# Twelve modulation units on another engine: from small TensorE matmuls in a scan loop to VectorE sums there and in the projection behind it

## The chip, the cores and the metric

The kernel runs on one core of a Trainium2 chip. The metric is the device time of one execution in microseconds (us), the median of the runs shown. The engines are named as in the profile: PE is TensorE (PEld its weight loads), DVE is VectorE, ACT is ScalarE, POOL is GpSimd and SP is SyncE, which here issues every load and store. All tensors are float32; large matmuls are made of three products of a rounded high part and a remainder (float32r).

## The reference, cut to what matters

Two transformer-like blocks over 256 positions of width 2048. In the first, a vector c is turned into six modulation rows of 2048 numbers, and these scale, shift and gate what follows:

```python
mod = jax.nn.silu(c) @ ada_w + ada_b
sh_m, sc_m, g_m, sh_f, sc_f, g_f = jnp.split((mod + ada_table[layer])[:, None, :], N_MOD, axis=-1)
h = _rms(x, norm_mix_pre[layer]) * (1 + sc_m) + sh_m
y, v_first = _rwkv7_mix(h, ...)
x = x + g_m * _rms(y, norm_mix_post[layer])
h = _rms(x, norm_ffn_pre[layer]) * (1 + sc_f) + sh_f
f = _conv_ffn(h, ...)
x = x + g_f * _rms(f, norm_ffn_post[layer])
```

`ada_w` has 2048 rows and 12288 columns, 100 MB in all. `_rwkv7_mix` projects h to r, k, v and some small hidden vectors, runs a recurrence with a 64 by 64 state for each of 32 heads over the 256 positions, and projects the outcome with `w_o`. `_conv_ffn` is a gated FFN of width 5504. The second block (attention, convolution and a gate) is not touched.

## The kernel before, in words

The program is written with a tile framework: the text allots tiles from pools, and the framework draws up each engine's queue, sets the semaphores and may take an instruction ahead of an earlier one whose operands or buffers are not free; what comes earlier in the text has the higher priority. So the order on an engine is near that of the text, but not the same.

**Modulation units.** A unit computes 512 columns of one modulation row (`k0` is the first of its four blocks of 128 columns; `seg` the row). A helper reads the 2048 x 512 part of `ada_w` in eight loads of 512 KB into the pool `adap` (three buffers in the stages that matter) and yields after every second load, so a unit has four steps. There are two helpers:

- `ada_group_pe` (lines 243 to 262) multiplies each 128 x 512 block on TensorE by a 128 x 32 tile whose first column is silu(c) (line 256, 16 matmuls a unit, two records each in the profile), copies the result from PSUM with ScalarE (line 260) and so makes a row.
- `ada_group` (lines 213 to 241) multiplies each block by silu(c) on VectorE and adds it to an accumulator `acc` of 128 x 512: the first block by line 232, the other 15 by line 238. Two other ways in it, on ScalarE and GpSimd, are switched off (`ada_pool[0] = 0`).

In both, `ada_fm` (lines 264 to 275) closes the unit: four matmuls with a column of ones (line 273) sum over the partitions into a column layout, and VectorE adds the bias (line 275). `ada_row` writes the 512 numbers to DRAM one by one (line 306), from where a later stage reads them as a row; `ada_scale` and `ada_shift` leave them in the tile `dv`. `ada_run(lag, ...)` chains units; it closes one when `lag` steps of the next have run, or at the next step when `lag` is 0.

**Stages.** First (to about 300 us) the norm, the modulation rows 0 and 1, and the k, v and low-rank products. Then the loop over q = 0 to 3 (lines 851 to 865), one pass for four pairs of heads:

```python
for i in range(4):
    for _ in operands(q * 4 + i, AR, BK, EC):
        for _ in range(SSTEP):
            next(sc, None)
        for _ in range(QSTEP):
            next(ada, None)
for _ in sc:
    pass
sc = scan(q, AR, BK, EC)
```

`operands` makes one pair's inputs of the scan and yields three times: after the low-rank part, after the r product (`fm_unit`, two `w_r` loads of 512 KB, split into high and remainder by ScalarE line 135 and VectorE line 139, 48 matmuls at lines 150 to 152), and at its end (lines 608 to 623). `scan(q)` runs as a generator beside the operands of pass q + 1: it starts with lines 690 and 693, solves 32 triangular systems by 30 serial steps of a multiply and an add on VectorE (lines 726 and 729), transposes (739, 742), and then goes through four chunks with matmuls, copies and a norm. `ada` is the run of twelve late units: rows 2 (units 0 to 3, the gate `g_m`, written to DRAM as `gmd`), 4 (units 4 to 7, scale of the FFN norm) and 3 (units 8 to 11, its shift). Before, each of the 48 yields takes one step, so all twelve units are done on TensorE in the loop.

After the loop, scan 3 runs beside `e_proj` and the first w_o products. The w_o product goes by four blocks `nb` of 512 columns (lines 980 to 998); `tm_out` evicts a block and multiplies it with the gate row `grow`, which is read back from `gmd` at line 994. Then come the residual (line 910), the norm, `to_fm` with the transposes, which needs the scales and shifts of units 4 to 11, and the FFN. In the FFN's loop over 43 blocks four more units (row 5, written as `gfd`) run with `ada_group` on VectorE, one step every third block.

Buffers: `NADA2 = 3` loads of `ada_w`, `NRAW = 4` weight loads and `NWHL = 2` splits in the loop, `NRAW2 = 5` and 3 afterwards.

Of the kernel before, what the change touches and what calls it, by code (L numbers as in the profile page):

```python
# [20 lines left out]
SSTEP, QSTEP = 3, 1  # L21
# [7 lines left out]
ADALAG = 2  # L29

GROUPS = ((0, 2), (2, 4), (6, 4), (10, 4), (14, 2))
P = 128
T = 256
D = 2048
KT = 16
# [23 lines left out]
def body(tc, A, out):  # L59
# [153 lines left out]
    def ada_group(seg, k0, nk, accs):  # L213
# [4 lines left out]
        for q in range(KT // n):  # L218
            raw = t_(adap[0], [P, 1024], "raw").rearrange("p (a c) -> p a c", c=w_)
            SP.dma_start(raw, A["ada_w"][q * n * P:(q + 1) * n * P, c0:c0 + w_].rearrange("(a p) c -> p a c", p=P))  # L220
            for a in range(n):
                b = q * n + a
                sc = sil[:, b:b + 1]
                w = 1 if b % 4 < ada_pool[0] else 0
                if accs[w] is None:
                    accs[w] = t_(accp[0], [P, 512], f"acc{w}", bufs=2 - w)
                acc = accs[w][:, :w_]
                if first[w]:
                    if w:
                        S.activation(acc, raw[:, a, :], AF.Copy, scale=sc)  # L230
                    else:
                        V.tensor_scalar(acc, raw[:, a, :], sc, None, op0=ALU.mult)
                elif w:
                    tp = t_(small, [P, 512], "nbr", bufs=1)[:, :w_]
                    S.activation(tp, raw[:, a, :], AF.Copy, scale=sc)
                    G.tensor_tensor(acc, acc, tp, op=ALU.add)
                else:
                    V.scalar_tensor_tensor(acc, raw[:, a, :], sc, acc, op0=ALU.mult, op1=ALU.add)
                first[w] = False
# [121 lines left out]
    def mix(m, k0, nk, dst, d0=0):  # L361

        mt = t_(pa, [P, 4, T], "mt", bufs=2)[:, :nk, :]
        for i in range(nk):
# [15 lines left out]
    ada = ada_run(ADALAG, *[ada_row(2, k0, 4, V_NMP, gmd) for k0 in range(0, KT, 4)],  # L380
                  *[ada_scale(4, k0, 4, D_AF, V_NFP) for k0 in range(0, KT, 4)],
                  *[ada_shift(3, k0, 4, D_BF) for k0 in range(0, KT, 4)])
# [146 lines left out]
    adap[0] = adx.enter_context(pool("adap2", NADA2, side="right"))  # L529
    phb = ExitStack()  # L530
# [16 lines left out]
    def operands(j, AR, BK, EC):  # L547

        w, i = divmod(j, 4)
        l2 = t_(pr, [P, 4, P], "l2", bufs=2)  # L550
# [300 lines left out]
    for q in range(4):  # L851
# [3 lines left out]
        for i in range(4):  # L855
            for _ in operands(q * 4 + i, AR, BK, EC):
                for _ in range(SSTEP):
                    next(sc, None)
                for _ in range(QSTEP):
                    next(ada, None)  # L860
# [3 lines left out]
    for _ in ada:  # L864
        pass
# [115 lines left out]
    for nb in range(4):  # L981
# [13 lines left out]
        elif nb == 1:  # L995
            V.tensor_copy(xt[:, 0, 0:1], accs(1)[0][:, 0:1])
            SP.dma_start(xt, A["x"].rearrange("(h p) d -> p h d", p=P))
        tm_out(po, accs(nb), nb, y2, grow, ssq)
# [13 lines left out]
    accp[0] = phf.enter_context(pool("accp", 2, reuse_waits="tile"))  # L1012
# [410 lines left out]
```

## Time and profile before

| | us |
|---|---|
| median of 3 runs | 2219.46 |
| lowest, highest | 2217.79, 2228.51 |
| the profiled execution's own time | 2202.98 |
| its span, first to last instruction | 2201.2 |

The profile is of one execution. Its page gives busy time by engine, the span in 40 slices with the granted TensorE clock, the DMA queues, the chain of work that ended last, and groups of instructions. In a group, "out<-in" names the tiles, "xcount" the instructions, then busy us and the mean ns of one, and behind the second bar the idle time of that engine just before them with what ended it. In the rows by stretches each engine has its busy us and, in brackets, its instructions; PEclk is the granted clock of TensorE as a share of 2.4 GHz, and the last two numbers are the DMA share and GB/s.

### The profile page before, as it was taken

The page shows a single profiled execution, that of the slowest core. Times are in us where ns is not written, and L with a number is a line of the kernel's source. Part 1 is how long each engine was busy: PE and PEld are TensorE (multiplying, and loading weights), DVE is VectorE, ACT ScalarE, POOL GpSimd, SP SyncE. Part 2 cuts the span into 40 slices and gives each one's busy share as a digit, 9 for nine tenths or more (in the row PEclk, how much of TensorE's full clock was granted, in tenths as well). Part 3 has the DMA queues.
Part 4 walks back from the last instruction along what each step waited for, and adds up shares of the span by engine and source line. Part 5 has one row for each costly group of instructions (what it writes and reads, how often), then busy time and mean ns, then how long its engine had stood idle before and what let it go on. Part 6 is the DMA issues. An engine that isn't in the chain of part 4 may idle for free.

```text
span 2201.2 us, 37566 instructions
## 1 busy us (share of the span) xinstructions
PE 2054.0 (93%) x15092; PEld 1728.1 (79%) x15092; DVE 1312.3 (60%) x2229; ACT 1001.7 (46%) x1554; POOL 387.7 (18%) x210
## 2 busy tenths in 40 slices
PE   6999977699999899799999999999998999999998
PEld 3778854466666467699999999978886889998887
DVE  3687873757676657866567676523336476665435
ACT  3544462234343444545544545434445444454453
POOL 1000000000000000122223222222332322322232
PEclk8999998889999989899999999999999999999999
DMA  8888656777664748665667566576664545556664
GB/s 291 297 297 283 206 199 205 200 200 217 197 209 152 207 150 303 212 193 180 185 183 248 181 213 190 175 233 193 191 196 135 177 144 175 170 165 219 191 197 153
DMA packets 192351, 446.36 MB, mean 203 GB/s; under 512 B 42792, under 2 KB 65448, under 8 KB 190896
## 3 DMA queue, kind: packets, MB, share of 16 engines
q1 hardware_dynamic: 192176, 443.96, 63.9%
q8 instruction: 118, 1.93, 0.4%
q14 instruction: 57, 0.47, 0.1%
HBM read 427.63 MB, written 16.27 MB: 202 GB/s over the span
## 4 chain that ended last, share of the span: by engine, by line
PE 81%; DMA 8%; DVE 6%; ACT 3%; issue 1%; SPq 0%; another core or an unknown queue 0%; POOL 0%; ACTq 0%; DVEq 0%; POOLq 0%
PE ps_s L150 6%; PE ps_s L152 6%; PE ps_s L151 6%; PE ps_g L150 5%; PE ps_g L152 5%; PE ps_g L151 5%; PE ps_a L256 4%; DMA raw<-in_ada_w 4%; PE ps_s L165 4%; PE ps_g L167 4%; PE ps_s L166 4%; PE ps_s L167 4%; PE ps_g L166 4%; PE ps_g L165 4%; DVE wlo L139 1%; PE ps_s L438 1%
## 5 line engine op out<-in xcount | busy, mean ns | idle before, releaser
L135 ACT ACTIVATE whi<-raw 128x1024 fp32r<-128x1024 f32 x562 | 594.0, 1058 | 741.7 <-issue 157.9
L139 DVE TENSOR_TENSOR wlo<-raw,whi 128x1024 fp32r<-128x1024 f32 x414 | 509.7, 1233 | 457.0 <-ACT whi L135 454.2
L139 POOL TENSOR_TENSOR wlo<-raw,whi 128x1024 fp32r<-128x1024 f32 x148 | 363.1, 2454 | 980.6 <-ACT whi L135 944.9
L150 PE MATMUL ps_g<-xh,whi 128*128 128x256 f32 x816 | 236.8, 290 | 14.7 <-ACT whi L135 14.7
L152 PE MATMUL ps_g<-xh,wlo 128*128 128x256 f32 x816 | 236.8, 290 | 3.0 <-DVE wlo L139 2.9
L151 PE MATMUL ps_g<-xl,whi 128*128 128x256 f32 x816 | 236.0, 289 | 0.0
L152 PE MATMUL ps_s<-xh,wlo 128*128 128x256 f32 x816 | 231.1, 283 | 2.7 <-DVE wlo L139 2.7
L150 PE MATMUL ps_s<-xh,whi 128*128 128x256 f32 x816 | 231.1, 283 | 0.0
L151 PE MATMUL ps_s<-xl,whi 128*128 128x256 f32 x816 | 230.9, 283 | 0.0
L150 PEld LDWEIGHTS ps_g<-xh,whi 128*128 128x128 f32 x816 | 160.5, 197 | 26.3 <-ACT whi L135 16.7
L256 PE MATMUL ps_a<-raw,sil 128*32 128x512 f32 (+1 forms) x704 | 139.7, 591 | 36.5 <-DMA raw<-in_ada_w 26.6
L152 PEld LDWEIGHTS ps_g<-xh,wlo 128*128 128x128 f32 x816 | 160.2, 196 | 13.0 <-issue 6.2
L151 PEld LDWEIGHTS ps_g<-xl,whi 128*128 128x128 f32 x816 | 160.4, 197 | 5.0 <-issue 4.2
L152 PEld LDWEIGHTS ps_s<-xh,wlo 128*128 128x128 f32 x816 | 156.6, 192 | 3.1 <-DVE wlo L139 3.1
L150 PEld LDWEIGHTS ps_s<-xh,whi 128*128 128x128 f32 x816 | 156.8, 192 | 0.0
L151 PEld LDWEIGHTS ps_s<-xl,whi 128*128 128x128 f32 x816 | 156.6, 192 | 0.0
L150 PE MATMUL ps_s<-h3h,whi 128*128 128x256 f32 x384 | 107.8, 281 | 0.0
L152 PE MATMUL ps_s<-h3h,wlo 128*128 128x256 f32 x384 | 106.6, 278 | 0.0
L151 PE MATMUL ps_s<-h3l,whi 128*128 128x256 f32 x384 | 106.2, 277 | 0.0
L256 PEld LDWEIGHTS ps_a<-raw,sil 128*32 128x32 f32 x704 | 23.3, 110 | 82.2 <-DMA raw<-in_ada_w 41.1
L150 PEld LDWEIGHTS ps_s<-h3h,whi 128*128 128x128 f32 x384 | 72.2, 188 | 3.6 <-issue 3.5
L152 PEld LDWEIGHTS ps_s<-h3h,wlo 128*128 128x128 f32 x384 | 72.3, 188 | 0.3 <-issue 0.3
(494 smaller groups left out, 4633.0 us busy)
## 6 DMA issues: line engine op xcount, KB each, us to landing
raw<-in_w_f SPq DMA_DIRECT2D x258, 512.0 KB, 4.5
raw<-in_ada_w SPq DMA_DIRECT2D x192, 512.0 KB, 5.4
raw<-in_w_i2f SPq DMA_DIRECT2D x80, 512.0 KB, 3.7
raw<-in_w_o SPq DMA_DIRECT2D x64, 512.0 KB, 4.8
raw<-in_w_v SPq DMA_DIRECT2D x32, 512.0 KB, 4.7
raw<-in_w_k SPq DMA_DIRECT2D x32, 512.0 KB, 4.8
raw<-in_w_r SPq DMA_DIRECT2D x32, 512.0 KB, 7.3
raw<-in_w_g SPq DMA_DIRECT2D x32, 512.0 KB, 4.8
```

The lines of the kernel that those rows point to most:

```text
L135: S.activation(hi, raw, AF.Copy)
L139: e.tensor_sub(lo, raw, hi)
L150: mm(acc, wh[:, sl], xh[:, kt, :], start=(kt == 0), stop=False)
L151: mm(acc, wh[:, sl], xl[:, kt, :], start=False, stop=False)
L152: mm(acc, wl[:, sl], xh[:, kt, :], start=False, stop=(kt == KT - 1))
L165: mm(a, xh, wh[:, sl], start=st, stop=False)
L166: mm(a, xl, wh[:, sl], start=False, stop=False)
L167: mm(a, xh, wl[:, sl], start=False, stop=sp_)
L256: mm(acc[r:r + 32, :w_], sil32[:, b, :], raw[:, a, :], start=(b < 4), stop=(b >= KT - 4))
L438: mm(acc[:, o], wl[:, sl], x[0][:, kt, :], start=False, stop=(i == 1 and kt == nk - 1))
```

## The change

All twelve late units use `ada_group` on VectorE (the list `ON_PE` of units that stay on TensorE is empty). In the loop over q only the first two of the three yields take a step, so 32 steps, eight units, remain there. The other four units take 4, 6 and 6 steps in the w_o product, ahead of the eviction of its blocks 0, 1 and 2. Their accumulator `acc` has one buffer, in a pool opened before the loop, and the FFN's four units use the same one, where they had a pool of their own with two. Units are closed at the next step (`ADALAG` 0 instead of 2). The small weight tile `l2` has one buffer instead of two.

```diff
-SSTEP, QSTEP = 3, 1
+SSTEP, QSTEP = 3, 2
+OSTEP = (4, 6, 6, 0)
+
+ON_PE = ()
...
-ADALAG = 2
+ADALAG = 0
...
-                    accs[w] = t_(accp[0], [P, 512], f"acc{w}", bufs=2 - w)
+                    accs[w] = t_(accp[0], [P, 512], f"acc{w}", bufs=1)
...
-    ada = ada_run(ADALAG, *[ada_row(2, k0, 4, V_NMP, gmd) for k0 in range(0, KT, 4)],
-                  *[ada_scale(4, k0, 4, D_AF, V_NFP) for k0 in range(0, KT, 4)],
-                  *[ada_shift(3, k0, 4, D_BF) for k0 in range(0, KT, 4)])
+    late = []
+    for u in range(12):
+        ada_how[0] = ada_group_pe if u in ON_PE else ada_group
+        k0 = u % 4 * 4
+        late.append(ada_row(2, k0, 4, V_NMP, gmd) if u < 4 else ada_scale(4, k0, 4, D_AF, V_NFP) if u < 8
+                    else ada_shift(3, k0, 4, D_BF))
+    ada = ada_run(ADALAG, *late)
...
     adap[0] = adx.enter_context(pool("adap2", NADA2, side="right"))
+    accp[0] = adx.enter_context(pool("accp", 1, side="right"))
...
-        l2 = t_(pr, [P, 4, P], "l2", bufs=2)
+        l2 = t_(pr, [P, 4, P], "l2")
...
-            for _ in operands(q * 4 + i, AR, BK, EC):
+            for e, _ in enumerate(operands(q * 4 + i, AR, BK, EC)):
                 for _ in range(SSTEP):
                     next(sc, None)
-                for _ in range(QSTEP):
+                if e < QSTEP:
                     next(ada, None)
...
-    for _ in ada:
-        pass
     wide_m[0] = True
...
+        for _ in range(OSTEP[nb]):
+            next(ada, None)
         tm_out(po, accs(nb), nb, y2, grow, ssq)
...
-    accp[0] = phf.enter_context(pool("accp", 2, reuse_waits="tile"))
     ada_how[0] = ada_group
```

## Rows read from the trace of the kernel before

**Rows 1.** The page's first part, busy us, share of the span, instructions.
```profile
PE 2054.0 (93%) x15092; PEld 1728.1 (79%) x15092; DVE 1312.3 (60%) x2229; ACT 1001.7 (46%) x1554; POOL 387.7 (18%) x210
```

**Rows 2.** Busy time by stretches of the loop, the scan tail, w_o and the residual.
```profile
300.00:415.00 115.00, 83.14 (x617) 55.12 (x616) 52.90 (x117) 39.16 (x77) 2.46 (x11) 0.85 0.74 229
415.00:523.00 108.00, 93.67 (x1025) 64.08 (x1024) 65.85 (x179) 45.78 (x94) 2.98 (x9) 0.92 0.75 197
523.00:632.00 109.00, 104.26 (x1097) 71.26 (x1097) 75.20 (x213) 45.59 (x94) 3.13 (x10) 0.97 0.67 204
632.00:740.00 108.00, 101.51 (x1090) 69.51 (x1089) 69.86 (x201) 39.31 (x81) 3.02 (x9) 0.97 0.59 176
740.00:837.00 97.00, 83.98 (x745) 56.09 (x739) 69.22 (x181) 42.20 (x81) 1.19 (x3) 0.91 0.59 178
837.00:896.00 59.00, 58.26 (x257) 47.90 (x256) 43.03 (x50) 26.10 (x33) 0.00 (x0) 1.00 0.90 318
896.00:945.00 49.00, 33.35 (x245) 31.76 (x244) 39.77 (x59) 29.96 (x58) 12.90 (x5) 0.83 0.58 196
```

**Rows 3.** The scans' first instruction, line 690: durations, first and last start.
```profile
L690 DVE TENSOR_TENSOR TQ<-ps_m,cst x7: 673/676/683, 398.3 to 740.2; 64x512 f32<-64x512 f32 x7
```

**Rows 4.** Groups of 300 to 740 us: modulation matmuls and closing matmuls.
```profile
L256 PE MATMUL ps_a<-raw,sil 128*32 128x512 f32 x384 | 98.2, 636 | 32.7 <-DMA raw<-in_ada_w 22.8 <-DVE AR L598 5.1 <-issue 2.7
...
L273 PE MATMUL ps_m<-cst,nbr 128*128 128x1 f32 x96 | 12.2, 248 | 0.7 <-ACT nbr L260 0.7
```

**Rows 5.** Waits of TensorE, 300 to 415 us: total, times, longest.
```profile
PE ps_g L150 <- ACT whi L135: 14.7, 3, 12.3
PE ps_a L256 <- DMA raw<-in_ada_w: 7.8, 2, 6.1
```

**Rows 6.** Load queue in order of time, around the first gate write.
```profile
344.90 0.43 SPq L306 DMA_DIRECT2D gmd<-adav  x1
...
346.50 8.90 SPq L250 DMA_DIRECT2D raw<-in_ada_w  x2
```

**Rows 7.** Chain of 340 to 412 us, its longest piece.
```profile
345.38 13.48 DMA raw<-in_w_r
```

**Rows 8.** Busy time: solve of q = 2, its rest, solve of q = 3's scan.
```profile
523.00:563.00 40.00, 36.82 (x240) 23.54 (x239) 35.97 (x136) 10.01 (x19) 0.26 (x2) 1.00 0.77 240
563.00:633.00 70.00, 68.39 (x866) 48.46 (x864) 40.22 (x80) 35.58 (x76) 2.87 (x8) 0.95 0.60 182
741.00:785.00 44.00, 33.07 (x138) 19.00 (x136) 36.77 (x128) 20.43 (x38) 0.15 (x1) 0.84 0.81 243
```

**Rows 9.** Line 238, the sums: minimum, median and maximum ns.
```profile
L238 DVE SCALAR_TENSOR_TENSOR acc<-raw,sil,acc x60: 642/749/2901, 826.5 to 1312.0; 128x512 f32<-128x512 f32 x60
```

**Rows 10.** VectorE in order of time: first FFN unit's start and closing.
```profile
825.97 0.48 DVE L232 TENSOR_SCALAR acc<-raw,sil 128x512 f32<-128x512 f32 x1
...
1141.31 0.16 DVE L275 TENSOR_TENSOR adav<-ps_m,vec 128x4 f32<-128x4 f32 x1 [1.35 <-PE ps_m L273]
```

**Rows 11.** Modulation matmuls (line 256) by stretches: PE busy, PEld busy, clock, DMA.
```profile
300.00:415.00 115.00, 23.57 (x104) 3.30 (x104) 0.85 0.74 229
...
523.00:563.00 40.00, 13.10 (x46) 1.85 (x46) 1.00 0.77 240
563.00:633.00 70.00, 12.77 (x52) 1.90 (x50) 0.95 0.60 182
```

**Rows 12.** Line 238 in 808 to 900 us: VectorE busy, clock, DMA.
```profile
808.00:900.00 92.00, 21.95 (x28) 1.00 0.76 261
```

**Rows 13.** All engines in order of time, behind w_o.
```profile
897.37 3.54 DVE L238 SCALAR_TENSOR_TENSOR acc<-raw,sil,acc 128x512 f32<-128x512 f32 x2 [1.28 <-DMA raw<-in_ada_w]
897.84 2.52 POOL L139 TENSOR_TENSOR wlo<-raw,whi 128x1024 fp32r<-128x1024 f32 x1 [89.08 <-ACT whi L135]
```

**Rows 14.** VectorE in order of time, in the solve of q = 2.
```profile
547.35 0.67 DVE L581 TENSOR_TENSOR_SCAN pc<-smask,thw 128x256 f32<-128x256 f32 x1
547.95 0.20 DVE L729 TENSOR_TENSOR XT<-XT,pt 64x77 f32<-64x77 f32 x1
```

## Prediction

> **What bounds the kernel now.** I read the page's busy line first, then the busy time by stretches, then the instruction groups and the waits of the stretch that the change empties. Over the span TensorE is busy 93% and VectorE 60% [rows 1]; this average hides the stages. The stretches [rows 2] are mine. The first scan starts at 398.3 us and the last at 740.2 [rows 3], so 300 to 415 is pass q = 0 of the loop with the first 17 us of q = 1, and the next three end where a scan starts; q = 3's scan runs beside the start of the w_o product until about 837, w_o goes on to 896, and the residual and transposes follow. In the passes TensorE is busy 83 of 115, 94 of 108, 104 of 109 and 102 of 108 us, VectorE 53, 66, 75 and 70. So TensorE looks like the bound of q = 1 to 3, and of w_o (58.3 of 59 us), and in q = 0 something else: it idles 32 us there.
>
> What the change takes away is the modulation matmul: in 300 to 740 us it holds TensorE for 98.2 us, and TensorE stands idle ahead of it for another 32.7, of which 22.8 for the landing of its weights [rows 4]. A reader who stops here forecasts 98 us or more. Two views speak against it. In q = 0, TensorE's idle time is more often a wait for the r product's own weights (14.7 us) than for the modulation's (7.8) [rows 5]. A large part of that is one pattern: a finished gate row unit writes 512 single numbers to DRAM, the next two w_r loads then take 13.48 us to land, and the load queue (SP) stands 8.9 us at its next issue [rows 6, 7]. The change keeps all four of these writes. And in q = 2 the triangular solve (523 to 563) has VectorE busy 35.97 of 40 us, a serial run of small instructions; there VectorE is as full as TensorE (36.82) [rows 8].
>
> **The change part by part.** One unit is 16 VectorE sums: 480 ns for the first, 749 for each other, so 0.48 + 15 x 0.749 = 11.7 us [rows 9, 10]. Eight units in the loop are 93.7 us, four in w_o 46.9.
>
> *q = 0.* Three units' matmuls, 23.57 us [rows 11], and their 7.8 us of waits go; two units' sums, 23.4 us, fall on a VectorE that idles 62 of 115 us, and eight loads of 512 KB fewer are issued. What stays is the wait for w_r. Unknown: how much of the 23.57 lay inside those waits. Ends: 23.57 + 7.8 = 31 us gained, or 13 lost, if one more write's stop falls into the gap. I take a gain of 14, three fifths of the matmul row.
>
> *q = 1 to 3.* q = 2 is the pattern. Outside the solve (563 to 633) TensorE is busy 68.39 of 70 us; 12.77 of it go, and 16 sums (12 us) find VectorE busy only 40.22 of 70, so they cost nothing there; without that cover they cost 12. Inside the solve TensorE's 13.10 us give nothing back, as VectorE sets the end; 16 sums are 12.0 us, of which its 4.0 idle us take a third, so the solve grows by 8.0. The half and half split follows today's units: 13.10 us in the solve, 12.77 outside [rows 8, 11]. Per pass 8.0 - 12.8 = -4.8. Ends: -12.8 if no sum enters the solve, 24 - 4 - 12.8 = +7 if all 32 do. I take -5 for q = 2 and q = 3, and -9 for q = 1, where I add a quarter of the 15 us (22.8 - 7.8) that TensorE waits for modulation weights after q = 0; the rest is handed to VectorE, which waits for the same landings.
>
> *The queue.* SP issues in order, and modulation loads wait for one of three buffers; a buffer now comes free by two sums (1.5 us) instead of two matmuls. Each step still issues two loads. Behind them stand the w_r loads, and ACT's split and the r product wait for those. I price that at nothing beyond the ends above.
>
> *Scan tail and w_o.* Four units come in: 46.9 us of sums. Today the stretch 808 to 900 carries 28 sums of the FFN's gate row units (21.95 us [rows 12]); they give way to the late units, which come earlier in the text, and move into the FFN, where TensorE is the bound. So VectorE gains about 25 us of work, against 27.8 + 16.0 idle us in 740 to 896. Loads: 64 sums need 32 loads (16.8 MB); today's 28 sums and two first ones need 15 (7.9 MB). The 8.9 MB more take 28 us at w_o's 318 GB/s, at a DMA share of 0.90 already; 740 to 837 runs at 178 GB/s and could take them all. Closing matmuls: 96 records for twelve units [rows 4], 1.0 us a unit; four move here and leave the loop. Ends: 0 and +28. I take +10: a third of the loads lands late.
>
> *Clock.* The solve of q = 2 ran at clock 1.00 with TensorE busy 36.8 of 40 us; q = 3's solve, 33.1 of 44, was granted 0.84, a mix of its two levels, 1.2 and 2.4 GHz [rows 8]. Without its modulation matmuls the solve of q = 2 has 23.7 of 40. If what follows falls from 0.95 to 0.84, its 55.6 us of TensorE work grow by 7.3 us, 22 over three passes; most of that is not on the chain any more. I take +4, with ends 0 and 22.
>
> *The rest.* One accumulator buffer instead of two, the sum closed at once in the FFN, one l2 buffer instead of two: nothing, since TensorE fills the FFN and l2 is wanted once in some 27 us. If the FFN's sums came late, the gate row would delay its second product.
>
> **Sum:** -14 - 9 - 5 - 5 + 10 + 4 = -19 us. The profiled execution took 2202.98 us around a span of 2201.2; it becomes 2184. The median of the runs is 16.5 us above the profiled one, so I give 2219.46 - 19 = 2200.5.
>
> **The rivals.**
>
> *Slower: the w_o units queue behind TensorE (2232).* Unit 7's closing matmuls stand behind block 0 of w_o in the text, and with one accumulator unit 8 cannot begin before them; likewise units 8 and 9 with block 1, 10 and 11 with block 2. If TensorE takes them only at a block's end, 16, 24 and 16 sums (12 + 18 + 12 = 42 us) stand ahead of the next block's eviction and splits: +42 in place of +10 makes +13. It decides from the point where unit 7 is closed after block 0. For it: the first FFN unit began its sums at 825.97 and was closed at 1141.31 [rows 10], some 300 us later and in the FFN's loop, where the text has it: a full TensorE did not take it ahead. Sums that slide past 896 also run beside GpSimd, where two took 3.54 us with a GpSimd subtraction over them [rows 13]. The Trainium skill, page "SBUF — State Buffer", section "SBUF: two separate sides", says that a VectorE instruction with two SBUF inputs and a GpSimd one that reads SBUF lock each other out for their whole length. The row agrees. Against it: the same sums at 826 to 896 fitted between w_o's splits.
>
> *No change: the solves draw the sums (2218).* VectorE's queue fills gaps of the solve with whatever is ready: between two solve steps stand single instructions of other work [rows 14]. With 24 of 32 sums in the solve a pass changes by 18 - 4 - 12.8 = +1 instead of -5: +18 in three, so -1. Against it: today's units split evenly.
>
> *No change: the clock (2218).* Nothing but the clock's far end, 22 in place of 4, makes -1. For it stands the 0.84 above; against it that q = 2 outside the solve is still busy for 55.6 of about 58 us. The Trainium skill, page "TensorE: Matmul & The Clock Gate", section "What's actually happening", says that the throttled clock is the default and that activity releases it; it speaks for this rival, and the two solves agree with it.
>
> *Faster: the units run ahead (2176).* The text's places are not the engines': sums of the FFN began at 825.97, in the scan tail [rows 10]. In q = 0 VectorE idles 62 us, which would take two units more. The solves then get some 24 sums fewer (-18) and w_o less (-6): -43. The change would then not do what it says, a spread over products and scans. Against it: the gate writes would all fall into q = 0, and one accumulator holds each unit until the one ahead is closed.
>
> **How the numbers follow.** Forecast 0.40, w_o queue 0.24, solves 0.17, clock 0.07, run ahead 0.12. About 0.5%, 11 us, is what a measurement of this kernel can tell from no change: below 2208 is faster, above 2231 slower. Each case has about 10 us of its own. Faster: 0.33 of the forecast, all of the last rival and 0.02 of the solves, 0.47. Slower: 0.16 of the w_o queue, 0.04 of the two at 2218, 0.02 of the forecast, 0.22. Same: 0.31. The range runs from 2165 (half of the last rival's spread below its centre) to 2242 (as much above the slower one); by itself the forecast has 2190 to 2212.
>
> **What would show it.** Modulation matmuls fall from 704 records to 320, sums rise from 64 to 256, VectorE's busy time between the first and the last scan start from 211 by 70 us. Right: q = 0 near 100 us, q = 2 near 104 with its solve at 48, w_o at most 10 longer. Wrong: w_o blocks apart by 30 us instead of 20 (three in 59 us), a solve beyond 55 us, a pass under 98, or VectorE waiting on modulation weights in the solve.

## The result, and the profile after

| | before | changed |
|---|---|---|
| median, us | 2217.79 (5 runs) | 2242.91 (5 runs) |
| lowest, highest | 2210.74, 2228.51 | 2233.99, 2244.91 |
| profiled execution | 2202.98 | 2244.91 |

The ratio is 1.0105, 95% interval 1.0081 to 1.0129: some 23 us slower, where 19 us faster was forecast, and 1 us outside the range. The profile of before is a quick one, 15 us under its median, so single stages are compared with several profiles below.

The first part of the changed kernel's page, and its row of granted clocks in 40 slices:

```profile
PE 2032.6 (91%) x14708; PEld 1768.1 (79%) x14708; DVE 1438.8 (64%) x2421; ACT 996.7 (44%) x1542; POOL 389.4 (17%) x210
...
PEclk8999997686777898799999999999999999999999
```

TensorE lost 21 us of busy time, though the change takes 98.2 us of modulation matmuls out of the loop [rows 4]; VectorE gained 127. Slices 7 to 14 (336 to 785 us, the loop) stand at 6 to 8 tenths of the clock. The counts are those forecast: 320 modulation records and 256 sums (16 first ones and 240).

```profile
L259 PE MATMUL ps_a<-raw,sil x320: 379/592/1062, 16.3 to 223.8; 128*32 128x512 f32 x96, 128*32 128x256 f32 x64
...
L241 DVE SCALAR_TENSOR_TENSOR acc<-raw,sil,acc x240: 640/745/2904, 312.2 to 1417.9; 128x512 f32<-128x512 f32 x120
```

The scans' first instruction (line 698 now) answers to [rows 3]: the first scan starts 24.6 us earlier, the last only 9.8 us earlier.

```profile
L698 DVE TENSOR_TENSOR TQ<-ps_m,cst x7: 671/672/681, 373.7 to 730.4; 64x512 f32<-64x512 f32 x7
```

Busy time by stretches, as in [rows 2, 8], now cut at the scans: to the first scan; then solve and rest of each of the passes q = 1 to 3 in turn; the last scan's solve; and w_o from its first eviction to the residual.

```profile
300.00:374.00 74.00, 48.40 (x408) 41.31 (x408) 56.97 (x100) 33.16 (x62) 2.30 (x10) 0.82 0.85 240
374.00:428.00 54.00, 32.40 (x180) 27.66 (x181) 47.97 (x159) 13.23 (x28) 0.26 (x2) 0.66 0.60 177
428.00:502.00 74.00, 65.29 (x835) 54.91 (x834) 49.58 (x90) 34.59 (x70) 2.87 (x8) 0.81 0.63 162
502.00:549.00 47.00, 29.08 (x168) 24.39 (x167) 45.72 (x156) 9.88 (x22) 0.25 (x2) 0.66 0.51 134
549.00:618.00 69.00, 67.21 (x830) 56.29 (x828) 48.36 (x88) 34.48 (x69) 2.86 (x8) 0.78 0.57 167
618.00:664.00 46.00, 27.07 (x169) 22.28 (x169) 45.24 (x156) 9.99 (x23) 0.26 (x2) 0.78 0.44 133
664.00:730.00 66.00, 64.27 (x796) 53.89 (x798) 45.89 (x84) 29.73 (x61) 2.75 (x7) 0.77 0.41 119
730.00:772.00 42.00, 30.71 (x162) 17.54 (x151) 35.48 (x131) 19.26 (x38) 0.15 (x1) 0.85 0.85 250
...
834.00:924.00 90.00, 70.33 (x266) 53.66 (x266) 66.61 (x87) 25.10 (x35) 0.72 (x1) 0.85 0.88 304
```

Two things are new. The solves lie at a clock of 0.66 to 0.78 and the stretches behind them at 0.77 to 0.81, and there TensorE is as full as before (67.21 of 69 us; before 68.39 of 70 [rows 8]) with 12.8 us less to do. And w_o takes 90 us from its first eviction to the residual, at nearly before's DMA share (0.88 against 0.90) and rate (304 GB/s against 318, [rows 2]), with TensorE idle for 20 of them.

w_o's evictions in the changed kernel, in order of time on VectorE (line 983; two row halves for each block):

```profile
834.45 0.69 DVE L983 TENSOR_TENSOR y<-ps_g,grow 128x512 f32<-128x512 f32 x1 [1.64 <-DMA grow<-gmd]
...
845.47 0.68 DVE L983 TENSOR_TENSOR y<-ps_s,grow 128x512 f32<-128x512 f32 x1
...
886.54 0.69 DVE L983 TENSOR_TENSOR y<-ps_g,grow 128x512 f32<-128x512 f32 x1 [1.94 <-PE ps_g L170]
...
920.84 0.69 DVE L983 TENSOR_TENSOR y<-ps_s,grow 128x512 f32<-128x512 f32 x1 [1.99 <-PE ps_s L170]
```

The first block is evicted 104 us behind the last scan's start, as before; then come gaps of 11, 41 and 34 us. In the kernel before they were 11, 20 and 19:

```profile
844.61 1.29 DVE L977 TENSOR_TENSOR y<-ps_g,grow 128x512 f32<-128x512 f32 x2 [0.53 <-DMA grow<-gmd]
856.08 1.28 DVE L977 TENSOR_TENSOR y<-ps_s,grow 128x512 f32<-128x512 f32 x2
875.97 0.68 DVE L977 TENSOR_TENSOR y<-ps_g,grow 128x512 f32<-128x512 f32 x1
...
895.39 0.69 DVE L977 TENSOR_TENSOR y<-ps_s,grow 128x512 f32<-128x512 f32 x1 [1.29 <-PE ps_s L167]
```

The waits of 834 to 924 us (total, times, longest) name the late one: ScalarE's split stands 51.1 us for `w_o` weights, where before it waited for TensorE's matmuls to free a buffer. First the changed kernel, then the one before (844 to 902 us):

```profile
ACT whi L138 <- DMA raw<-in_w_o: 51.1, 15, 9.3
...
ACT whi L135 <- PE ps_s L166: 13.5, 9, 1.7
```

The load queue shows why. What SP itself waited for longest in 834 to 924 us is that a sum on VectorE (line 241) frees a buffer for an `ada_w` load (line 223):

```profile
SPq L223 <- DVE acc L241: 46.8, 24, 4.7
```

The `w_o` loads stand behind those. In this piece of the queue, in order of time, six of them leave, one or three at a time, between groups of two or three `ada_w` loads:

```profile
858.32 3.60 SPq L223 DMA_DIRECT2D raw<-in_ada_w  x3
862.02 0.42 SPq L135 DMA_DIRECT2D raw<-in_w_o  x1
865.01 6.08 SPq L223 DMA_DIRECT2D raw<-in_ada_w  x3
871.18 1.37 SPq L135 DMA_DIRECT2D raw<-in_w_o  x3
873.31 3.52 SPq L223 DMA_DIRECT2D raw<-in_ada_w  x3
876.88 0.50 SPq L135 DMA_DIRECT2D raw<-in_w_o  x1
883.05 1.94 SPq L223 DMA_DIRECT2D raw<-in_ada_w  x2
885.09 0.42 SPq L135 DMA_DIRECT2D raw<-in_w_o  x1
```

### The profile page after: what moved, and what is told of

It reads as the page before. It is cut to its first block, busy times and chain, and to the rows that moved or that the text cites. A ratio compares the mean times of both kernels' runs of the same rounds, so it can differ in the third digit from the quotient of the medians.

```text
span 2243.1 us, 37054 instructions
## 1 busy us (share of the span) xinstructions
PE 2032.6 (91%) x14708; PEld 1768.1 (79%) x14708; DVE 1438.8 (64%) x2421; ACT 996.7 (44%) x1542; POOL 389.4 (17%) x210
## 4 chain that ended last, share of the span: by engine, by line
PE 74%; DVE 12%; DMA 9%; ACT 2%; issue 2%; SPq 0%; another core or an unknown queue 0%; POOL 0%; ACTq 0%; DVEq 0%; POOLq 0%
PE ps_s L153 6%; PE ps_s L155 6%; PE ps_s L154 5%; PE ps_g L153 5%; PE ps_g L155 5%; PE ps_g L154 5%; PE ps_g L170 4%; PE ps_g L168 4%; PE ps_g L169 4%; PE ps_s L168 4%; PE ps_s L169 4%; PE ps_s L170 3%; DMA raw<-in_ada_w 3%; DVE acc L241 3%; DVE wlo L142 2%
## 5 line engine op out<-in xcount | busy, mean ns | idle before, releaser
L153 PE MATMUL ps_g<-xh,whi 128*128 128x256 f32 x816 | 241.0, 295 | 18.5 <-ACT whi L138 18.5
L241 DVE SCALAR_TENSOR_TENSOR acc<-raw,sil,acc 128x512 f32<-128x512 f32 x240 | 201.3, 839 | 25.5 <-DMA raw<-in_ada_w 23.5
L153 PE MATMUL ps_g<-h3h,whi 128*128 128x256 f32 x256 | 72.9, 285 | 0.0
L155 PEld LDWEIGHTS ps_s<-h3h,wlo 128*128 128x128 f32 x384 | 72.3, 188 | 0.3 <-issue 0.3
```

Source lines behind the costliest of these rows:

```text
L153: mm(acc, wh[:, sl], xh[:, kt, :], start=(kt == 0), stop=False)
L155: mm(acc, wl[:, sl], xh[:, kt, :], start=False, stop=(kt == KT - 1))
```

## The experiments

All stages at a glance, from the starts of instructions in each profile: 300 us to the first scan, first to last scan, last scan to the residual, residual to the end. The ratio is to the kernel before, with its interval. A stage differs by 8 to 12 us between two profiles of the same text (c1_ffnonly has the loop of the kernel before, and its 350.3 stands against 341.9; a3_narrow has that of the changed kernel, 344.3 against 356.7), so less is not read from one.

The scans are counted from line 698 (690), which works in two halves. The solve can start only when both are done, with the transpose of line 701 (693). In most profiles that is 1 to 5 us later. In a2_engine, a7_q0 and b4_best, which have three units on VectorE in the first pass, the second half comes late there: the first solve starts 101.8, 97.9 and 98.7 us after 300 (before 100.2, c1_ffnonly 98.5), and in a2_engine the last one 481.1 us after 300, not 465.9. The first solve's transpose, first in the kernel before, then in a7_q0:

```profile
L693 DVE STREAM_TRANSPOSE NT<-TQ x4: 1936/1941/1989, 400.2 to 741.5; 64x1024 f32<-64x1024 f32 x4
...
397.90 1.93 DVE L701 STREAM_TRANSPOSE NT<-TQ 64x1024 f32<-64x1024 f32 x1
```

| kernel | ratio | to 1st scan | scans | to residual | to end |
|---|---|---|---|---|---|
| before | 1 | 98.3 | 341.9 | 161.4 | 1299.7 |
| changed | 1.0105 [1.0081, 1.0129] | 73.7 | 356.7 | 193.2 | 1319.5 |
| a1_place | 1.0064 [1.0043, 1.0084] | 73.4 | 333.5 | 206.6 | 1318.5 |
| a2_engine | 1.0133 [1.0091, 1.0174] | 90.6 | 375.3 | 169.5 | 1315.8 |
| a3_narrow | 1.0095 [1.0066, 1.0125] | 69.5 | 344.3 | 193.0 | 1317.8 |
| a4_noload | 0.9929 [0.9900, 0.9957] | 73.2 | 350.1 | 168.4 | 1312.8 |
| a5_tail | 1.0050 [1.0020, 1.0079] | 75.8 | 347.1 | 187.2 | 1316.8 |
| a6_fill | 1.0110 [1.0038, 1.0181] | 73.6 | 348.8 | 193.0 | 1313.5 |
| a7_q0 | 1.0023 [0.9995, 1.0051] | 86.6 | 342.9 | 164.8 | 1314.8 |
| b1_narrowloop | 1.0059 [1.0038, 1.0081] | 78.7 | 339.1 | 191.8 | 1320.3 |
| b2_ffn | 1.0097 [1.0070, 1.0124] | 72.3 | 346.0 | 192.2 | 1319.7 |
| b3_gpq | 1.0050 [1.0030, 1.0070] | 72.1 | 346.0 | 177.0 | 1326.0 |
| b4_best | 0.9970 [0.9950, 0.9991] | 87.4 | 348.3 | 160.7 | 1308.2 |
| c1_ffnonly | 0.9970 [0.9942, 0.9998] | 96.6 | 350.3 | 156.9 | 1310.0 |
| c2_fillrest | 1.0507 [1.0482, 1.0531] | 79.3 | 436.0 | 192.7 | 1314.0 |
| c3_steps | 0.9998 [0.9974, 1.0022] | 76.4 | 357.6 | 160.8 | 1315.0 |
| c4_fill128 | 1.0181 [1.0144, 1.0218] | 74.3 | 369.8 | 195.6 | 1314.6 |
| c5_fillnarrow | 1.0259 [1.0210, 1.0308] | 77.3 | 383.8 | 191.9 | 1316.1 |

**Place and engine apart.** The change moves the units and gives them to another engine. a1_place does the first alone, a2_engine the second.

```diff
a1_place:
-ON_PE = ()
+ON_PE = tuple(range(12))
```

> The changed kernel's places (32 steps in the loop, 16 in w_o), but all twelve units on TensorE as before. Theory (clock): in q = 1 to 3 the granted clock comes back to 0.95 and more, the passes fall to about 100 us from 112 to 128, the last scan starts near 710 us instead of 730. Rival (the clock is a bystander, the scan's own chain sets the pass): the clock comes back but the last scan starts at 725 or later. Theory (loads): w_o stays 30 us or more above the kernel before, as its 32 loads are still there, plus up to 33 us of matmuls; total 2235 to 2250. Rival (sums delay w_o): w_o within 15 us of before and the total below 2215.

```diff
a2_engine:
-SSTEP, QSTEP = 3, 2
-OSTEP = (4, 6, 6, 0)
+SSTEP, QSTEP = 3, 3
+OSTEP = (0, 0, 0, 0)
...
+    for _ in ada:
+        pass
```

> All twelve units on VectorE, but at the places of before: three steps a pair in the loop, nothing in w_o. Theory (clock eats the gain in the loop): the last scan starts 5 to 20 us later than before (740), with the clock in q = 1 to 3 below 0.85; w_o and the rest as before; total 2220 to 2240. Rival (VectorE sums are cheaper than the matmuls, and only w_o made the change slow): the last scan starts at 725 or earlier, total below 2205.

Each alone is slower than the kernel before. The place is what shortens the start (73.4 with TensorE as with VectorE) and what lengthens w_o (206.6, more than with VectorE). The engine costs in the loop. From 300 us to the last scan a1_place takes 73.4 + 333.5 = 406.9; the changed kernel, with the same eight units on VectorE, 430.4, and five profiles with that loop unchanged (a3, a4, a5, b2, b3) 413.8 to 423.3. With twelve units, a2_engine takes 465.9 (to the solve 481.1) against 440.2 before and 446.9 in c1_ffnonly (to the solve 441.5 and 448.2). So a unit costs some 1 to 3 us more on VectorE, though by busy time VectorE had room for it; the low end lies within the scatter. a2_engine is slower than its expectation allowed (median 2250 us, 2220 to 2240 expected).

**w_o: sums or loads.** a3_narrow keeps the late loads and nearly takes their sums away; a4_noload keeps the sums and takes seven of eight loads away.

```diff
a3_narrow, units 8 to 11:
-V.scalar_tensor_tensor(acc, raw[:, a, :], sc, acc, op0=ALU.mult, op1=ALU.add)
+V.scalar_tensor_tensor(acc[:, :16], raw[:, a, :16], sc, acc[:, :16], op0=ALU.mult, op1=ALU.add)
```

> The changed kernel with 15 of the 16 sums of units 8 to 11 over 16 columns instead of 512, so that w_o keeps every load and closing but little VectorE work (this leaves out most of those four units' result). Theory (loads): w_o's third block still ends 35 to 42 us behind the second, total 2235 to 2245. Rival (sums): blocks 20 us apart, total near 2212.

```diff
a4_noload, units 8 to 11:
-raw = t_(adap[0], [P, 1024], "raw")...
-SP.dma_start(raw, A["ada_w"]...)
+if q == 0 or not once:
+    raw = t_(adap[0], [P, 1024], "raw")...
+    SP.dma_start(raw, A["ada_w"]...)
```

> The changed kernel with one load instead of eight for each of units 8 to 11, all 16 sums reading that one (this leaves out seven eighths of those units' weights). Theory (loads): w_o's blocks go back to 20 to 23 us apart, total 2205 to 2215. Rival (sums): blocks stay 30 us or more apart, total 2235 to 2245.

Without sums nothing comes back (193.0 to the residual); without loads 25 of the 32 us do (168.4), and the kernel is 0.7% faster than before. In a3_narrow ScalarE still waits for the weights, in a4_noload for TensorE, as before. The waits from first eviction to residual, first of a3_narrow:

```profile
ACT whi L138 <- DMA raw<-in_w_o: 45.4, 11, 22.9
```

and of a4_noload:

```profile
ACT whi L138 <- PE ps_s L169: 15.0, 11, 1.7
ACT whi L138 <- PE ps_g L169: 12.4, 7, 2.9
```

**w_o: bandwidth or order.** b3_gpq issues the same late loads from GpSimd's queue, so that SP's `w_o` loads stand behind none of them.

```diff
b3_gpq, units 8 to 11:
-SP.dma_start(raw, A["ada_w"]...)
+G.dma_start(raw, A["ada_w"]...)
```

> The changed kernel with the loads of units 8 to 11 issued by GpSimd, which is idle there, instead of SP's queue. Theory A (the order in SP's queue: w_o's loads stand behind modulation loads that wait for a buffer): blocks 20 to 25 us apart, total 15 us or more below the changed kernel. Theory B (bandwidth: twice the bytes in the same time): blocks stay 30 us or more apart, total within 8 us of the changed kernel.

177.0 us to the residual: 16 of the 25 us that a4_noload gave back are there with every load done, so two thirds of what the loads cost, half of w_o's 32 us, is the order in one queue. The other half is not taken apart; w_o runs at 342 GB/s there, at a DMA share of 0.94. Behind the residual 6 of the 16 us are lost again in this profile (1326.0 against 1319.5). The waits for free buffers now stand in GpSimd's queue, and ScalarE waits for TensorE again:

```profile
POOL raw L223 <- DVE acc L241: 55.9, 19, 7.1
ACT whi L138 <- PE ps_s L169: 17.5, 10, 3.9
```

**The late units in the scan tail.** The tail had bandwidth to spare [rows 2]; a5_tail gives it the sixteen late steps.

```diff
a5_tail:
-OSTEP = (4, 6, 6, 0)
+OSTEP = (0, 0, 0, 0)
...
     for e, _ in enumerate(sc):
+        if e >= 11:
+            next(ada, None)
```

> The changed kernel with the 16 late steps taken in the last scan's second half instead of in w_o, so that unit 7 is closed and units 8 to 11 are loaded before block 0 ends. Theory (place of the closing and loads): the stretch from the last scan's start to the residual falls from 193 us to 165 to 175, total 2215 to 2225. Rival (the sums then delay the scan as much): total 2238 or more.

187.2 us to the residual, far above the 165 to 175 that were expected. The last scan's part behind its solve grew from 51 to 81 us, and w_o shrank from 101 to 62: most of the loss only moves ahead of w_o. The total gains half a per cent on the changed kernel.

**The loop: sums.** b1_narrowloop makes 15 of 16 sums of units 0 to 7 narrow, as a3_narrow did for the late ones.

```diff
b1_narrowloop, units 0 to 7:
-V.scalar_tensor_tensor(acc, raw[:, a, :], sc, acc, op0=ALU.mult, op1=ALU.add)
+V.scalar_tensor_tensor(acc[:, :16], raw[:, a, :16], sc, acc[:, :16], op0=ALU.mult, op1=ALU.add)
```

> The changed kernel with 15 of the 16 sums of units 0 to 7 over 16 columns instead of 512, so that the loop keeps all its loads, steps and closings but little VectorE work of the units (this leaves out most of those units' result). TensorE is then no busier than in the changed kernel, so its clock stays low. Theory (the sums on VectorE take the loop's gain): the last scan starts at 705 or earlier instead of 723 to 730, total 15 to 25 us below the changed kernel. Rival (the low clock takes it): the last scan starts at 715 or later, total within 10 us of the changed kernel.

The solves shorten by 8, 4 and 8 us (46.8, 42.8 and 38.4, from 54.6, 47.0 and 46.4), the total by 10 us. But the rests stay at 77, 68 and 66 us, at clocks of 0.80, 0.85 and 0.81, though neither engine has much modulation work left; in a1_place, with all of it on TensorE, they take 63, 64 and 63 at 1.00, 0.89 and 0.84. So the sums are not what holds the rests. The place of the loads is not excluded by this: in a1_place's third rest the DMA share is 0.20, in b1_narrowloop's 0.41.

**The loop: the clock.** Four kernels put idle matmuls on TensorE, whose result nobody reads, to hold its clock up.

```diff
a6_fill, scans 0 to 2, at each of ten points of the solve:
+fill = ps("a")
+for _ in range(3):
+    mm(fill, ident, cst[:, 0:512], start=True, stop=True)
```

> The changed kernel with three idle matmuls (128 x 128 by 512, results never read) at each of ten points of the solves of q = 0 to 2, to keep TensorE busy there. Theory (clock): granted clock in the three solves and behind them at 0.95 and more, the part of a pass outside the solve 58 to 62 us instead of 66 to 73, total 2215 to 2228. Rival (the scan's chain sets the pass, not the clock): the clock comes back and the passes stay at 112 to 128 us, total 2240 or more.

Ratio 1.011, as without them. The first two solves ran at 1.00 and were hardly shorter (52 and 46 us; the third was not filled, as its idle matmuls ran ahead into the stretch before 374). But the rows behind the second solve, which ended at 545, show that this tested the solve alone: some 10 us later the clock is down again, at a busy TensorE.

```profile
536.00:546.00 10.00, 7.16 (x43) 5.37 (x44) 10.00 (x31) 1.06 (x1) 0.00 (x0) 1.00 0.61 189
546.00:556.00 10.00, 8.20 (x156) 7.74 (x155) 9.51 (x9) 3.40 (x5) 0.10 (x1) 0.72 0.50 164
556.00:566.00 10.00, 9.93 (x83) 7.52 (x83) 2.44 (x5) 3.93 (x10) 0.52 (x1) 0.50 0.45 150
```

```diff
c2_fillrest, in place of a6_fill's:
+def idle(w, x):
+    if q < 3:
+        mm(ps("a"), w, x, start=True, stop=True)
...
+for _ in range(3):
+    idle(NT[:, 0:4, :]..., cst[0:64, 0:512])
...
+idle(ident[0:32, :], T1...[:, 0:512])
...
+if c < 2:
+    idle(ident, Gt[:, 0:4, :]...)
```

The last two stand behind the solve: twice at its end, and at each step of the first two chunks. c4_fill128 and c5_fillnarrow (the latter on top of b1_narrowloop) have 128 rows in the solve, and `Gt` in both places behind it:

```diff
-idle(NT[:, 0:4, :]..., cst[0:64, 0:512])
+idle(ident, AR[:, 3]...)
...
-idle(ident[0:32, :], T1...[:, 0:512])
+idle(ident, Gt[:, 0:4, :]...)
```

> The changed kernel with idle 128-row by 512-column float32 matmuls on TensorE, whose result nobody reads: three at each of the ten points of the solve of scans 0 to 2, as before but tied to the scan's own data so that they cannot run ahead, and new ones behind the solve, two at its end and one at each of the first six steps of the chunks (eight, some 10 us of TensorE work at full clock). If the clock behind the solve is what lengthens the passes, the granted clock of the stretches between a solve's end and the next scan start rises from 0.77 to 0.81 to 0.93 or more, and each of them falls from 66 to 74 us to 60 to 65 in spite of the added work, the total by 8 to 20 us (ratio 0.99 to 0.997 to the changed kernel, 1.001 to 1.007 to the kernel before). If the clock is a bystander, the stretches stay or grow by up to 10 us each at the higher clock, ratio 1.011 to 1.022. If the clock stays near 0.5 behind the solve in spite of them, the question stays open.

c2_fillrest is not what its expectation says: the edit has 64 rows in the solve and 32 at its end, not 128. It settles nothing: TensorE was busy 65.5 of 72 us in the first solve, at a clock of 0.72, with 871 ns for each record of the idle matmuls in 374 to 560 us, and 300 us to the last scan took 85 us more than in the changed kernel.

> As c2_fillrest, but all idle matmuls have 128 rows: three at each of the ten points of the solve, reading the last pair's operands of the scan, two at the solve's end and one at each of the first six steps of the chunks. Clock theory: with the solve and the 30 us behind it at 0.95 or more, the stretch from a solve's end to the next scan start falls from 74, 69 and 66 us to 60 to 66, and from 300 us to the last scan start it takes 405 to 415 us in place of 418 to 430; ratio to the kernel before 1.000 to 1.007. Rival, the clock is a bystander: stretches as long as in the changed kernel or up to 10 us longer, 420 to 455 us, ratio 1.010 to 1.022. If the clock behind the solve stays under 0.85, it tests nothing.

c4_fill128 is the test: the clock is 1.00 in all three solves, and 0.87, 1.00 and 0.97 behind them. The rest of q = 2 in c4_fill128, and of it the idle matmuls (line 724: PE busy, PEld busy, clock, DMA):

```profile
560.00:628.00 68.00, 63.43 (x859) 50.12 (x857) 48.88 (x90) 37.10 (x72) 2.86 (x8) 1.00 0.56 168
```

```profile
560.00:628.00 68.00, 9.06 (x18) 2.48 (x17) 1.00 0.56 168
```

The real work there now holds TensorE 63.43 - 9.06 = 54.4 us, where the changed kernel needed 67.21: the low clock had cost 12.8 us in this rest, as much as the modulation matmuls that were taken out. The stretch is 68 us, between the two theories' numbers: of the 12.8 us the idle matmuls take 9, TensorE idles 3 longer, and 1 is gained. The third rest is no shorter either (66 us at 0.97, as at 0.77), and the first is 80 us (at 0.87). From 300 us to the last scan it takes 444.1 us, at a ratio of 1.0181: these are the rival's numbers. So holding the clock up in this way pays nothing; what it shows is TensorE's 12.8 us, not a shorter pass.

The price is seen without idle matmuls, too. c1_ffnonly has the loop of the kernel before, and in its profile the clock fell once behind a solve. That rest, first in the kernel before:

```profile
673.00:740.00 67.00, 63.74 (x853) 45.63 (x851) 34.37 (x66) 29.81 (x63) 2.76 (x7) 0.97 0.49 141
```

and in c1_ffnonly:

```profile
673.00:747.00 74.00, 70.52 (x858) 49.90 (x857) 34.92 (x68) 29.80 (x63) 2.76 (x7) 0.88 0.45 133
```

The same matmuls take 63.74 us at 0.97 and 70.52 at 0.88 (63.74 x 0.97 / 0.88 = 70.3), and the rest is 7 us longer.

The profiles that share the changed kernel's loop say the same. Its rest of q = 2 took 69 us at 0.78 and that of q = 3 66 us at 0.77; here are q = 2's in b3_gpq and q = 3's in a5_tail, 5 us shorter each, with TensorE nearly as full (96% against 97%):

```profile
544.00:608.00 64.00, 61.16 (x829) 51.92 (x829) 48.27 (x88) 33.90 (x69) 2.86 (x8) 0.88 0.60 183
...
662.00:723.00 61.00, 58.40 (x810) 49.37 (x810) 45.18 (x84) 29.58 (x61) 2.75 (x7) 0.87 0.42 125
```

So part of the scatter in the loop goes with the clock, and the profile of the changed kernel is the case with the lowest: in the others TensorE needed 61 to 63 us for the rest of q = 2, 7 to 9 more than the 54.4 at the full clock.

> The same idle matmuls in the kernel whose units 0 to 7 have 15 of their 16 sums over 16 columns only (their rows are not computed whole). Without the idle matmuls it took 417.8 us from 300 to the last scan start, with the stretches behind the solves at 0.80 to 0.85, though TensorE and VectorE have less to do than with eight units as TensorE matmuls (406.9 us). Clock theory: 395 to 407 us, ratio 0.994 to 1.002. Rival, bystander (the loads or the queue set it): 417 to 440 us, ratio 1.006 to 1.017.

c5_fillnarrow missed both numbers, with 461 us from 300 to the last scan. In its shorter solves (50, 49 and 37 us) the idle matmuls found no room; they slid into the rests (91, 80 and 77 us, TensorE busy for 79, 77 and 74 of them, at 0.89 to 0.98). It measures its own idle work and tells nothing apart.

**What q = 0 gained.** a7_q0 puts three units on VectorE in q = 0 and leaves nine on TensorE, at before's places; c3_steps keeps TensorE and takes one unit from q = 0 to q = 3.

```diff
a7_q0:
-SSTEP, QSTEP = 3, 2
-OSTEP = (4, 6, 6, 0)
-ON_PE = ()
+SSTEP, QSTEP = 3, 3
+OSTEP = (0, 0, 0, 0)
+ON_PE = tuple(range(3, 12))
c3_steps: ON_PE = tuple(range(12)), OSTEP zero, and
+SSTEP, QSTEP = 3, (2, 3, 3, 4)
...
+for _ in range((QSTEP[q] + 2 - e) // 3):
     next(ada, None)
```

> Units 0 to 2 (the first pass) on VectorE, the other nine on TensorE, all at the places of before. Theory (in q = 0 VectorE is free and TensorE's matmuls only add to the wait for weights): the first scan starts 10 to 20 us earlier than before (398), the rest as before, total 2198 to 2208. Rival (q = 0 gained from its eight loads fewer, not from the engine): the first scan starts within 5 us of before, total 2213 to 2222.

> The changed kernel with all twelve units on TensorE, all in the loop, but 8, 12, 12 and 16 steps in the four passes in place of the 12 each of the kernel before: two units in q = 0 and four in q = 3, none in the projection. If q = 0's gain comes from the two units there, the first scan starts 72 to 77 us after 300 (98 before), the last scan start to the residual stays at 157 to 165 us, and the pass of q = 3 grows by up to 13 us (one unit of 16 matmuls, 12.8 us on a full TensorE): total 8 to 15 us below the kernel before, ratio 0.993 to 0.997. If a unit taken out of q = 0 costs as much later (24 us in q = 3's pass, or stops of the load queue), the ratio is 0.999 to 1.003.

With three units on VectorE the first scan's first half starts at 86.6 us, but its solve at 97.9, within 3 us of the two profiles with three units on TensorE (100.2 and 98.5). With two units it starts at 76.2 and 79.2 with TensorE (a1_place, c3_steps) and at 71.6 to 78.1 with VectorE (the changed kernel and the five profiles with its loop). So q = 0's some 22 us are the unit's that left it, and the engine has next to no part in them, as the rival of a7_q0's expectation had it. Which part of the unit counts, its eight loads or its gate write (one falls into q = 0 in place of two), is not told apart. And c3_steps gives the 22 us back: its next pass takes 140.3 us (124.3 before), with three gate writes in it (392.8, 444.7 and 496.3 us) where two fell before, and the total is that of before.

**The FFN.** b2_ffn gives the changed kernel the FFN settings of before (two accumulators, lag 2); c1_ffnonly gives the kernel before those of the change.

```diff
b2_ffn:
+accp[0] = phf.enter_context(pool("accp2", 2, reuse_waits="tile"))
-ada = ada_run(ADALAG, *[ada_row(5, k0, ...)...])
+ada = ada_run(2, *[ada_row(5, k0, ...)...])
```

> The changed kernel with the FFN's settings of before: its own accumulator pool with two buffers and units closed two steps late. Theory (those settings cost the FFN one stop more): from the residual to the second product's first eviction 588 to 593 us instead of 603, total 7 to 12 us below the changed kernel. Rival (the FFN is covered by TensorE): total within 4 us of the changed kernel.

> The kernel before, with the FFN settings of the change alone: its four units use one accumulator buffer and are closed at the next step (lag 0). Loop, scan tail and w_o are those of the kernel before, so this is also a second profile of them, and shows how far stage times scatter between profiles. If the settings carry the loss behind the residual (1319.5 against 1299.7 us from the residual to the end in the two profiles), this run shows 1310 us or more there and a ratio of 1.006 to 1.009. If only one more stop at a gate write is lost, it is 6 to 8 us, a ratio of 1.003. If the settings cost nothing and 1299.7 was a low profile, the ratio is 1.000 (within 0.002) with 1305 to 1312 us there. Loop from first to last scan start: 342 (within 4), last scan start to residual 161 (within 4).

Neither shows a cost that can be told from none (1.0097 against 1.0105, and 0.997). A third pair does: a7_q0 and b4_best below differ in these settings alone, and stand at 1.0023 [0.9995, 1.0051] and 0.9970 [0.9950, 0.9991], each to its own runs of the kernel before. The pairs disagree, so a cost of up to some 10 us stays open. Half of the 20 us between the two first profiles behind the residual is the quick profile of before: c1_ffnonly has 1310.0 there, and runs at 0.997.

**The best version.** b4_best is a7_q0 with the FFN settings of before.

> Units 0 to 2 on VectorE and the other nine on TensorE, all at the places of before, and the FFN's settings of before. Theory (q = 0 gains some 10 us from VectorE, and only the FFN's settings gave them back): 0.3 to 0.6% below the kernel before. Rival (the 10 us at the first scan are given back later in the loop): within 0.2% of the kernel before.

Its 0.997 [0.995, 0.9991] is the best of the kernels that do the whole computation, but c1_ffnonly has the same ratio. It is no gain to build on, and since q = 0 gained nothing from the engine, the 0.5% below a7_q0 is not explained.

## Why the prediction was wrong

By stages, forecast against measured, by the means of the profiles with the same text in a stage: two of before (before and c1_ffnonly, which has the FFN settings of the change and so is not quite the same text in the last row), four to six of the change (in the scans 348.4 us against 346.1):

| | forecast | measured |
|---|---|---|
| to the first scan | -14 | -25 |
| q = 1 to 3, clock included | -9 - 5 - 5 + 4 = -15 | +2 |
| tail and w_o | +10 | +33 |
| behind the residual | 0 | +12 |

These sum to -19 and +22; the medians say +25.

**Scan tail and w_o: the step that failed most.** The forecast took "a third of the loads lands late". All but three of the 32 did. Unit 7 was closed at 819 us, behind w_o's first block, and with one accumulator and three buffers units 8 to 11 could not load more than three ahead of that; so hardly any of the scan tail's free bandwidth was used (144 GB/s in 772 to 834). The loads' price was near the forecast's far end, 8.9 MB at w_o's rate, 28 us: a4_noload gave 25 back. The bytes came, too: 90 us at 304 GB/s are 27.4 MB where 59 us at 318 were 18.8. The sign that the forecast named, blocks 30 us apart, is in the profile (41 and 34). The rival "the w_o units queue behind TensorE" had the place, the sign, the point of decision and nearly the total (2232), but its price was made of sums, and a3_narrow shows that these cost nothing. The load queue, which the forecast priced "at nothing beyond the ends above", is two thirds of what the loads cost (b3_gpq).

**The clock: the term that was mis-sized.** It was set at +4 with a far end of 22, since "most of that is not on the chain any more". The rests ran at 0.77 to 0.81, lower than the 0.84 of that far end, and in q = 2 TensorE needed 12.8 us more for the same work. The forecast's first half held there: 67.21 x 0.78 = 52.4 us at full clock against 68.39 x 0.95 = 65.0 [rows 8], the 12.6 us of the modulation matmuls. They were gone, and in this profile the clock took their time back. The Trainium skill, page "TensorE: Matmul & The Clock Gate", section "What's actually happening", has the low clock as the default that activity lifts; c4_fill128 agrees, where idle matmuls stand in the place of the units' wide ones, but c2_fillrest's first solve, busy for 65.5 of 72 us at 0.72, does not. That the passes are as long as before because of the clock is shown as far as the rests shorten with it in one text (69 us at 0.78, 64 at 0.88); c4_fill128 itself did not shorten them. What stays open is how short a rest would be at a full clock that costs nothing: that wasn't tried.

**The solves: right.** q = 2's took 47.0 us, where 48 was forecast. It drew 13 of the sums, not 24, with VectorE busy 45.72 of 47 us, so the rival "the solves draw the sums" falls. b1_narrowloop got 4 to 8 us back for each solve, the price that was forecast for q = 2.

The sums (line 241) in the second solve and its rest, VectorE busy, clock, DMA:

```profile
502.00:549.00 47.00, 9.57 (x13) 0.66 0.51 134
549.00:618.00 69.00, 12.49 (x17) 0.78 0.57 167
```

**q = 0: right in sign, for another reason.** The forecast's 14 us were three fifths of the matmuls' row. But three units on VectorE gain next to nothing there (a7_q0); the gain is the unit that left q = 0, and it came with TensorE as well (a1_place, c3_steps). That the term had the right sign was in part luck: the forecast names the eight loads fewer, but gives them no price. The wait for `w_r` stayed, as forecast: TensorE waits 18.5 us for it in 300 to 391 us, where it was 14.7 [rows 5].

```profile
PE ps_g L153 <- ACT whi L138: 18.5, 4, 10.9
```

**The rest: open.** For one accumulator and lag 0 in the FFN, priced at nothing, two pairs show no cost and one shows half a per cent. Of the 12 us behind the residual at most 4 are unit 11, which is closed at 948 us, 25 behind the residual's start, while the FFN's norm needs it (the norm's eighth output starts 29.4 us behind the residual, 25.6 before and 27.8 in c1_ffnonly); the others are not accounted for. The rival "the units run ahead" falls: unit 7 began its sums at 702 us, in the last pass, where the text has it.

## What to carry to other kernels

Work that looks like a load on a full engine can be what keeps that engine's clock up: before taking wide matmuls away, look at what is left in the stretches where the chain waits for small instructions of another engine. Work moved beside a stage that runs at full DMA share brings its bytes along, and in an in-order queue also its waits for buffers; count both before its arithmetic, and issue such loads from another queue. Choose a mark that the stage's next work really waits for: the first half of a scan's start came 11 us before its solve could begin. And profile a stage twice before believing a dozen us of it.

## What the runs showed that was not expected

TensorE kept busy did not always have the full clock: in c2_fillrest's first solve, with idle matmuls of 64 rows, it was busy 65.5 of 72 us at 0.72, a mix of its two levels, while in c4_fill128's, with 128 rows and the same 512 columns, it was busy 52.9 of 55 us at 1.00. The number of rows is not the whole answer: in c2_fillrest's third solve the same 64-row matmuls ran at 0.96. What decided is open. The first solve of c2_fillrest, that of c4_fill128, and the third of c2_fillrest:

```profile
379.00:451.00 72.00, 65.51 (x221) 31.90 (x222) 49.55 (x161) 13.43 (x28) 0.28 (x3) 0.72 0.48 143
```

```profile
374.00:429.00 55.00, 52.91 (x250) 29.98 (x249) 50.37 (x163) 13.88 (x29) 0.28 (x3) 1.00 0.64 191
```

```profile
693.00:745.00 52.00, 51.30 (x210) 26.38 (x209) 44.62 (x154) 9.68 (x21) 0.25 (x2) 0.96 0.40 124
```

And much of the scatter between runs of one kernel goes with the mean granted clock: over the 12 runs of c1_ffnonly the span lies between 2197.5 and 2216.1 us and the clock between 0.968 and 0.961, with a correlation of -0.72. The profile of before, a quick one, stood at 0.968, the highest of that range.
